# The last gate product of a two-block layer: steps between weight splits, partial sums kept in PSUM banks, the last block product by token block

## The chip, the cores and the metric

One core of a Trainium2 chip. The metric is device time in microseconds, the median of several runs. All times below are microseconds unless marked ns. The engines are named as in the profile: PE (TensorE, matmul), PEld (its weight loads), DVE (VectorE), ACT (ScalarE), POOL (GpSimd), SP (SyncE, which only issues transfers here).

## What is computed

Two layers on 512 tokens of width 2048, in float32. The first is a recurrence beside latent attention, the second sparse attention beside spatial gating. Only the end of the second layer changes:

```python
def second_block(x, p, ..., w_ple, w_ple_gate, final_g):
    ...
    x = x + merged @ w_out[l]
    x = x + jax.nn.sigmoid(x @ w_ple_gate[l]) * (p[l] @ w_ple[l])
    return rms_norm_2(x, final_g)

def rms_norm_2(x, g):
    xf = x.astype(jnp.float32)
    y = xf * lax.rsqrt(jnp.mean(xf * xf, axis=-1, keepdims=True) + EPS)
    return (y * g.astype(jnp.float32)).astype(x.dtype)
```

`x @ w_ple_gate` is 512x2048 by 2048x2048. `p @ w_ple` was computed earlier and lies in DRAM (`ple_d`).

## The kernel before

**Splitting.** A float32 weight block comes by DMA as `wraw`, ACT copies it into `whi` (a rounded format), DVE subtracts to get `wlo`. The same is done with the left operands. `mm3` then makes three matmuls, hi*hi, lo*hi and hi*lo, into one bank. A weight block of 128x2x512 is a *unit*; the list of all units is the `spine`. At each unit the program issues up to `LD = 4` fetches and `LS = 3` splits ahead.

**Seven block products.** The last product is done by a scheme of Strassen's kind, for two *pairs* p of column blocks, c = 2p and 2p + 1, 512 columns each. The left operand is cut in four quarters: two halves of the tokens (rows) by two halves of the inner dimension. Per pair there are seven block products, in the order `PROD = ("1","7","6","2","5","3","4")`. The left operands are the *forms* `F[q, k]`: sums of quarters (through `fs`), split. The weights' sums were made earlier by accumulating DMAs of POOL (`ws0x...`). Each product has four units, each unit 12 matmuls of 128x512: two token blocks j, two k, three of `mm3`. A product of token blocks j = 0, 1 has one bank per j (`pg1`, `pg7`, ...).

**Putting together.** `after_prod(p, q, j)` runs when the bank of (q, j) is done: `q1` is a copy of product 1 by ACT; `w = P6 - q1`; `q1 + P2` is a result; then `e = P5 + w`, `c22 = e - P7` is a result, `w = P7 - w`; `e + P3` and `w + P4` are results. A result is one 128x512 block (token block b of 4, column block c of 4) of the gate's argument. `gated` takes it on: tanh on ACT (`tgate`), two `stt` on DVE (with `plel`, which is p @ w_ple, and with `x3`, the residual x), a square with a sum into `ssq` on ACT. `scaled` multiplies `x3` by the final gain `fg` on DVE. In the code all of that is one piece: the whole of it stands in the queues of ACT and DVE where `after_prod` is called, with no split of weights between its steps.

**Order.** Work beside the spine is written as generators (`sides`); each `yield` names tiles, and `pump` goes on with a generator when a clock of estimates says that those are ready by then and that DVE and ACT are not too far behind PE. The list of instructions so found is then fixed by hand-made dependencies for every engine, so each engine's queue holds exactly that order.

**The end.** `finish(b, sums)` sums the squares of a token block, takes the reciprocal root by integer and Newton steps of 128x1 on DVE (tile `part`), scales the four column blocks of `x3` (ACT and DVE) and issues four output DMAs, from the queues of SP, ACT, SP and POOL. For token blocks 2 and 3, `part_gen` sums three of the four squares ahead. Product 4 of pair 1 is last (`last_product`). Its units are kept until all four are there; then j = 0 is computed 512 wide, j = 1 as two halves of 256, each half into a bank of its own:

```python
            for s in (slice(0, 512),) if j == 0 else (slice(0, 256), slice(256, 512)):
                ps = bank("pg4")[:, s]
```

In the rows, L285 is `tt` (DVE, two tensors), L304 `stt` (DVE, tensor, scalar and tensor), L294 and L296 `ts`, L316 `act`, L322 `mm`, L330 `dma`. After the change these are L283, L302, L292 and L294, L314, L321 and L329. The banks are named `pg` in the rows, with all buffers under one name; `q` is `q1`, `c` is `c22`, `x` is `x3`.

Of the kernel before, what the change touches and what calls it, by code (L numbers as in the profile page):

```python
# [12 lines left out]
OP = mybir.AluOpType  # L13
# [68 lines left out]
THIN = False  # L82
# [154 lines left out]
class Unit:  # L237
    def __init__(self, src, shape, mm, pre=None, hold=1, half=False, thin=False):


        self.src, self.shape, self.mm, self.pre, self.hold, self.half = src, shape, mm, pre, hold, half
        self.thin = thin
        self.raw = self.hi = self.lo = None


def emit(ctx, tc, I, out):
# [74 lines left out]
    def mm(o, l, r, start, stop_):  # L321
        T.matmul(o, l, r, start=start, stop=stop_)  # L322
# [18 lines left out]
    def mm3(o, lh, ll, rh, rl, start=False, stop_=False):  # L341
        mm(o, lh, rh, start, False)
        mm(o, lh, rl, False, False)
        mm(o, ll, rh, False, stop_)
# [1073 lines left out]
    done = {"oa": [], "ob": [], "sg": [], "x2": 0}  # L1418
# [622 lines left out]
    def form(q, k, x):  # L2041
        t = slot([128, 2, 256], "F" + q, F32R)
        act(t[:, 0], x, AF.Copy)
        yield [t]
        tt(t[:, 1], x, f(t[:, 0]), OP.subtract)
        F[q, k] = t

    def early_forms(k):
        x11, _, x21, x22 = quarters(k)
        yield [x22]  # L2050
        yield from form("1", k, x11)
# [5 lines left out]
        yield from form("6", k, s[:, 1])  # L2057

    def late_forms():
        for k in range(8):  # L2060
# [62 lines left out]
    def gated(b, c, src, s=slice(0, 512), end=False):  # L2123

        x = x3[b, c][:, s]
        t = slot([128, 512], "tgate")[:, s]
        act(t, src, AF.Tanh, scale=0.5)
        stt(t, t, 1.0, pl_[b, c][:, s], OP.add, OP.mult)
        stt(x, t, 0.5, x, OP.mult, OP.add)
        o = ssq[:, b, c:c + 1]  # L2130
        if end:
            o = small("sqe")[:, 0:1]
            stt(t, x, 1.0, x, OP.mult, OP.mult, accum_out=o)
        else:
            act(t, x, AF.Square, accum_out=o)
        return o

    def scaled(b, c):
        x = x3[b, c]
        tt(x, x, pl_["fg", c], OP.mult)  # L2140

    def after_prod(p, q, j):

        c = 2 * p
        ps = acc[q, j] if q == "7" else acc.pop((q, j))
        if q == "1":
            t = tmp["1", j] = slot([128, 512], "q1")
            act(t, ps, AF.Copy)
        elif q == "6":
            w = tmp["w", j] = slot([128, 512], "wq")  # L2150
            tt(w, ps, tmp["1", j], OP.subtract)
        elif q == "2":
            t = tmp.pop(("1", j))
            tt(t, ps, t, OP.add)
            gated(j, c, t)
        elif q == "5":
            e, t, w, p7 = slot([128, 512], "eq"), slot([128, 512], "c22"), tmp["w", j], acc.pop(("7", j))
            tmp["e", j] = e
# [249 lines left out]
```

## Time and profile before

| what | value |
|---|---|
| median of 3 runs | 2417.43 (2416.79 to 2417.78) |
| the profiled execution | 2413.85 |
| its span | 2412.0 |
| mean granted clock of PE | 0.992 |
| PE busy in the span | 2349.8 (97%) |
| DVE, ACT, POOL busy | 1543.5 (64%), 971.2 (40%), 290.5 (12%) |
| the stage that changes: first matmul to the end of the span | 2200.29 to 2412.0 |

The page's rows give, for an engine, its busy time and share; a mean over the whole span says little of the last stage, so the rows further down are read from that stretch alone. In a timeline row, the first number is the start from the span's start, the second the time taken, and the bracket behind it the idle time of that engine just before and what ended it.

### The profile page before, as it was taken

The numbers are of one execution on the slowest core, as the hardware profiler recorded it, in microseconds if no ns is written. First come the engines' busy times: TensorE is split into PE (matmuls) and PEld (weight loads), VectorE is DVE, ScalarE is ACT, GpSimd is POOL, SyncE is SP. The second block draws the span as 40 slices with busy tenths as digits, with TensorE's granted clock in tenths as the row PEclk, the third lists the DMA queues.
The fourth block names the chain that finished last, engine by engine and source line by source line (L and its number), as shares of the span: only waits on it lengthen the run. The fifth ranks groups of instructions, "written<-read, shape, count | busy, mean of one in ns | idle before, by whom it ended". The sixth has DMA issues, their size and how long they took to land.

```text
span 2412.0 us, 30852 instructions
## 1 busy us (share of the span) xinstructions
PE 2349.8 (97%) x11323; PEld 1965.0 (81%) x11323; DVE 1543.5 (64%) x2928; ACT 971.2 (40%) x1785; POOL 290.5 (12%) x432
## 2 busy tenths in 40 slices
PE   8999999999999999999999999999999999999895
PEld 6778889888888987888888888888888888888674
DVE  6777988788855377468887347776243444335766
ACT  6333366555543343344444235444232222224443
POOL 0000031432312002000000100001012000111110
PEclk9999999999999999999999999999999999999897
DMA  9976732432355346434444634435456433445563
GB/s 347 362 258 241 248 124 71 131 125 94 123 183 165 104 151 173 146 114 123 126 114 136 170 109 123 119 114 143 130 195 220 128 114 113 132 141 194 186 233 131
DMA packets 124167, 383.10 MB, mean 159 GB/s; under 512 B 16542, under 2 KB 16836, under 8 KB 123504
## 3 DMA queue, kind: packets, MB, share of 16 engines
q1 hardware_dynamic: 94896, 273.41, 34.7%
q0 software_dynamic: 28256, 106.58, 15.0%
q8 instruction: 89, 1.46, 0.2%
q10 hardware_dynamic: 864, 1.14, 0.1%
q14 instruction: 62, 0.51, 0.1%
HBM read 343.32 MB, written 71.30 MB: 172 GB/s over the span
## 4 chain that ended last, share of the span: by engine, by line
PE 53%; issue 6%; DVE 3%; ACT 1%; POOL 1%; DMA 0%; POOLq 0%; DVEq 0%; ACTq 0%
PE pch L322 45%; PE pO L322 2%; PE psc L322 2%; PE pPT L326 1%; PE pg L322 1%; DVE wlo L285 1%; ACT whi L316 0%; DVE cA L285 0%; PE pcs L322 0%; PE px L326 0%; DMA w1r<-in_cmp_w_v_dram 0%; DVE vx L304 0%; POOL x L330 0%; POOL plel L330 0%; PE psv L322 0%
## 5 line engine op out<-in xcount | busy, mean ns | idle before, releaser
L285 DVE TENSOR_TENSOR wlo<-wraw,whi 128x1024 fp32r<-128x1024 f32 (+5 forms) x421 | 498.0, 1184 | 190.6 <-ACT whi L316 188.1
L316 ACT ACTIVATE whi<-wraw 128x1024 fp32r<-128x1024 f32 (+5 forms) x423 | 424.2, 1013 | 321.8 <-PE pch L322 120.4
L322 PE MATMUL pch<-h2h,whi 128*128 128x512 f32 x1216 | 483.2, 397 | 0.0
L322 PE MATMUL pch<-h2h,wlo 128*128 128x512 f32 x1216 | 474.9, 391 | 0.0
L322 PE MATMUL pch<-h2l,whi 128*128 128x512 f32 x1216 | 474.5, 390 | 0.0
L322 PEld LDWEIGHTS pch<-h2h,wlo 128*128 128x128 f32 x1216 | 228.2, 188 | 48.4
L322 PEld LDWEIGHTS pch<-h2l,whi 128*128 128x128 f32 x1216 | 228.9, 188 | 41.0
L322 PEld LDWEIGHTS pch<-h2h,whi 128*128 128x128 f32 x1216 | 228.6, 188 | 41.0
L322 PE MATMUL pg<-whi,F 128*128 128x512 f32 (+1 forms) x464 | 149.4, 403 | 21.3 <-ACT whi L316 14.6
L316 ACT ACTIVATE P<-psc,sm 128x512 f32<-128x512 f32 (+3 forms) x160 | 83.7, 527 | 134.1 <-DVE sm L308 103.8
L322 PEld LDWEIGHTS pg<-whi,F 128*128 128x128 f32 x464 | 91.4, 200 | 43.4 <-ACT whi L316 17.2
L322 PE MATMUL pp<-hh,whi 128*128 128x512 f32 x320 | 126.0, 394 | 0.2 <-DVE acc L285 0.2
L322 PE MATMUL pp<-hh,wlo 128*128 128x512 f32 x320 | 124.7, 390 | 0.0
L322 PE MATMUL pp<-hl,whi 128*128 128x512 f32 x320 | 124.6, 389 | 0.0
L322 PE MATMUL pch<-mgh,whi 128*128 128x512 f32 x256 | 101.1, 395 | 0.0
L322 PE MATMUL pch<-mgh,wlo 128*128 128x512 f32 x256 | 99.9, 390 | 0.0
L322 PE MATMUL pch<-mgl,whi 128*128 128x512 f32 x256 | 99.6, 389 | 0.0
L322 PE MATMUL pch<-oh,whi 128*128 128x512 f32 x256 | 99.6, 389 | 0.0
L322 PE MATMUL pch<-ol,whi 128*128 128x512 f32 x256 | 99.6, 389 | 0.0
L322 PE MATMUL pch<-oh,wlo 128*128 128x512 f32 x256 | 99.6, 389 | 0.0
L322 PE MATMUL pg<-wlo,F 128*128 128x512 f32 (+1 forms) x232 | 93.8, 404 | 4.2 <-DVE wlo L285 4.2
L316 ACT ACTIVATE PTh<-pPT 128x512 fp32r<-128x512 f32 (+1 forms) x120 | 59.6, 529 | 90.9 <-PE pPT L326 88.5
(526 smaller groups left out, 4602.0 us busy)
## 6 DMA issues: line engine op xcount, KB each, us to landing
wraw<-in_w_in_dram SPq DMA_DIRECT2D x199, 512.0 KB, 3.6
wada<-in_w_mod_dram SPq DMA_DIRECT2D x128, 256.0 KB, 5.4
wraw<-in_w_out_dram SPq DMA_DIRECT2D x64, 512.0 KB, 3.6
wgate<-in_w_gate_dram SPq DMA_DIRECT2D x64, 256.0 KB, 4.6
wraw<-in_w_ple_gate_dram SPq DMA_DIRECT2D x24, 512.0 KB, 3.6
ws0x<-in_w_ple_gate_dram POOLq DMA_DIRECT2D x16, 512.0 KB, 7.6
ws1x<-in_w_ple_gate_dram POOLq DMA_DIRECT2D x16, 512.0 KB, 6.4
sg<-mg POOLq DMA_DIRECT2D x32, 256.0 KB, 2.6
```

The costliest lines, as they stand in the source:

```text
L285: V.tensor_tensor(o, a, b, op=op)
L316: A.activation(o, a, fn, **k)
L322: T.matmul(o, l, r, start=start, stop=stop_)
L326: T.transpose(o, a, i)
```

## The change

The last stage is written anew in four respects.

- *Generators.* `after_prod` now only copies (`q1`, `wq`) or spawns a generator (`from_2`, `from_5`, `from_3`, `from_4`); `gated` yields between tanh, `stt` and square. The gains `fg` on the columns of pair 0 are a generator too (`first_gains`), and `finish` of any block waits for its end. `finish` of blocks 0 and 1 is spawned when their four squares are noted (`nsum`).
- *Sums in the banks.* Form 1 is made with the scale -1, and products add up in a bank: 1, 6, 5 in bank `b`, 7 and 4 in `e`, 2 in `a`, 3 in `c`, with a start only for 1, 7, 2, 3. ACT copies what is needed on the way (`q1`, `wq`, `eq`), and DVE makes one addition or subtraction per result. Per pair and j, ACT has two copies more, DVE three operations fewer.
- *Form 2* of the first `EARLY2 = 4` k is made with the early forms, while `merged @ w_out` still runs.
- *The last product* is computed as its units come, token block 0 first; then token block 1 in two halves of 256, which are now two halves of one bank.

The part that goes with `thin` (never switched on) is dropped as well and left out here.

```diff
@@ -79,7 +79,7 @@
 SEGS = ((0, 0), (8, 1024), (16, 3136))
 EARLY = (0, 1, 8, 9)
 VGL = (((4656, 5016),), ((5016, 5376),), ((5376, 5680), (2560, 2608)))
-THIN = False
+EARLY2 = 4
 SUMS = 150
@@ -318,8 +316,9 @@
-    def mm(o, l, r, start, stop_):
-        T.matmul(o, l, r, start=start, stop=stop_)
+    def mm(o, l, r, start, stop_, on=False):
+        T.matmul(o, l, r, start=start, stop=stop_, skip_group_check=on)
@@ -2038,26 +2037,31 @@
         a, c = x2r[k], x2r[k + 8]
         return a[:, 0:256], c[:, 0:256], a[:, 256:512], c[:, 256:512]
-    def form(q, k, x):
+    def form(q, k, x, scale=1.0):
         t = slot([128, 2, 256], "F" + q, F32R)
-        act(t[:, 0], x, AF.Copy)
+        act(t[:, 0], x, AF.Copy, scale=scale)
         yield [t]
-        tt(t[:, 1], x, f(t[:, 0]), OP.subtract)
+        if scale == 1.0:
+            tt(t[:, 1], x, f(t[:, 0]), OP.subtract)
+        else:
+            stt(t[:, 1], x, scale, f(t[:, 0]), OP.mult, OP.subtract)
         F[q, k] = t
     def early_forms(k):
-        x11, _, x21, x22 = quarters(k)
+        x11, x12, x21, x22 = quarters(k)
         yield [x22]
-        yield from form("1", k, x11)
+        yield from form("1", k, x11, -1.0)
         s = slot([128, 2, 256], "fs")
         tt(s[:, 0], x11, x21, OP.subtract)
         tt(s[:, 1], s[:, 0], x22, OP.add)
         yield [s]
         yield from form("7", k, s[:, 0])
         yield from form("6", k, s[:, 1])
+        if k < EARLY2:
+            yield from form("2", k, x12)
     def late_forms():
-        for k in range(8):
+        for k in range(EARLY2, 8):
             yield
             yield from form("2", k, quarters(k)[1])
         for k in range(8):
@@ -2120,63 +2124,84 @@
         dma("G", pl_[b, c], ple_d[b][c])
         dma("G", x3[b, c], x2_d[:, b, c * 512:(c + 1) * 512])
-    def gated(b, c, src, s=slice(0, 512), end=False):
+    def gated(b, c, src, s=slice(0, 512), end=None):
+        yield [src, x3[b, c], pl_[b, c]]
         x = x3[b, c][:, s]
         t = slot([128, 512], "tgate")[:, s]
         act(t, src, AF.Tanh, scale=0.5)
+        yield [t]
         stt(t, t, 1.0, pl_[b, c][:, s], OP.add, OP.mult)
         stt(x, t, 0.5, x, OP.mult, OP.add)
-        o = ssq[:, b, c:c + 1]
-        if end:
-            o = small("sqe")[:, 0:1]
-            stt(t, x, 1.0, x, OP.mult, OP.mult, accum_out=o)
-        else:
-            act(t, x, AF.Square, accum_out=o)
-        return o
-    def scaled(b, c):
-        x = x3[b, c]
-        tt(x, x, pl_["fg", c], OP.mult)
+        if end is not None:
+            stt(t, x, 1.0, x, OP.mult, OP.mult, accum_out=end)
+            return
+        yield [x]
+        act(t, x, AF.Square, accum_out=ssq[:, b, c:c + 1])
+        if c > 1 and (b < 2 or c == 3):
+            tt(x, x, pl_["fg", c], OP.mult)
+        pl_.pop((b, c))
+        nsum[b] += 1
+        if b < 2 and nsum[b] == 4:
+            yield [ssq]
+            sides.spawn(finish(b, ()))
+        if b > 1 and nsum[b] == 3:
+            sides.spawn(part_gen(b))
+    nsum = [0] * TB
+    def first_gains():
+        for c in range(2):
+            for b in range(TB):
+                yield [x3[b, c]]
+                tt(x3[b, c], x3[b, c], pl_["fg", c], OP.mult)
+        done["gains"] = True
     def after_prod(p, q, j):
         c = 2 * p
-        ps = acc[q, j] if q == "7" else acc.pop((q, j))
         if q == "1":
             t = tmp["1", j] = slot([128, 512], "q1")
-            act(t, ps, AF.Copy)
+            act(t, acc["b", j], AF.Copy)
         elif q == "6":
-            w = tmp["w", j] = slot([128, 512], "wq")
-            tt(w, ps, tmp["1", j], OP.subtract)
-        elif q == "2":
-            t = tmp.pop(("1", j))
-            tt(t, ps, t, OP.add)
-            gated(j, c, t)
-        elif q == "5":
-            e, t, w, p7 = slot([128, 512], "eq"), slot([128, 512], "c22"), tmp["w", j], acc.pop(("7", j))
-            tmp["e", j] = e
-            tt(e, ps, w, OP.add)
-            tt(t, e, p7, OP.subtract)
-            tt(w, p7, w, OP.subtract)
-            gated(2 + j, c + 1, t)
+            t = tmp["w", j] = slot([128, 512], "wq")
+            act(t, acc["b", j], AF.Copy)
+        elif q in "25":
+            sides.spawn({"2": from_2, "5": from_5}[q](j, c))
         elif q == "3":
-            t = tmp.pop(("e", j))
-            tt(t, ps, t, OP.add)
-            gated(j, c + 1, t)
+            sides.spawn(from_3(j, c))
         elif q == "4":
-            t = tmp.pop(("w", j))
-            tt(t, ps, t, OP.add)
-            gated(2 + j, c, t)
-        if p == 1:
-            if q in "253":
-                b, cc_ = {"2": (j, c), "5": (2 + j, c + 1), "3": (j, c + 1)}[q]
-                scaled(b, cc_)
-            if q == "3":
-                sides.spawn(finish(j, ()))
-            if q == "5":
-                sides.spawn(part_gen(2 + j))
+            sides.spawn(from_4(j, c))
+    def from_2(j, c):
+        t, ps = tmp.pop(("1", j)), acc.pop(("a", j))
+        yield [t, ps]
+        tt(t, ps, t, OP.subtract)
+        yield from gated(j, c, t)
+    def from_5(j, c):
+        e, t, ps, p7 = slot([128, 512], "eq"), slot([128, 512], "c22"), acc.pop(("b", j)), acc["e", j]
+        tmp["e", j] = e
+        yield [ps]
+        act(e, ps, AF.Copy)
+        yield [e, p7]
+        tt(t, e, p7, OP.subtract)
+        done["c22"] += 1
+        yield from gated(2 + j, c + 1, t)
+    def from_3(j, c):
+        t, ps = tmp.pop(("e", j)), acc.pop(("c", j))
+        yield [t, ps]
+        tt(t, ps, t, OP.add)
+        yield from gated(j, c + 1, t)
+    def from_4(j, c):
+        t, ps = tmp.pop(("w", j)), acc.pop(("e", j))
+        yield [t, ps]
+        tt(t, ps, t, OP.subtract)
+        yield from gated(2 + j, c, t)
+    CH = {"1": "b", "6": "b", "5": "b", "7": "e", "4": "e", "2": "a", "3": "c"}
     OUT = {"2": (0, 0), "5": (2, 1), "3": (0, 1), "4": (2, 0)}
     def prod_pre(p, q, u):
@@ -2193,9 +2218,10 @@
                 for c in range(4):
                     t = pl_["fg", c] = slot([128, 512], "fg")
                     dma("G", t, bcast(I["final_g_2"], 512, c * 512))
-            if p == 1 and q in "762":
-                for b, c in {"7": ((0, 0), (1, 0)), "6": ((2, 1), (3, 1), (0, 1)), "2": ((1, 1), (2, 0), (3, 0))}[q]:
-                    scaled(b, c)
+            if p == 1 and q == "7":
+                sides.spawn(first_gains())
+            if q == "4":
+                sides.until(lambda: done["c22"] == 2 * p + 2)
             if q in OUT:
                 sides.until(lambda: done["x2"] == KT)
                 b, c = OUT[q]
@@ -2211,18 +2237,17 @@
             def mmf(hi, lo):
                 if last_:
                     held[u] = (hi, lo)
-                    if u == 3:
-                        yield from last_product(held)
+                    yield from last_product(u, held)
                     return
                 for j in range(2):
-                    if u == 0:
-                        acc[q, j] = bank("pg" + q)
-                    ps = acc[q, j]
+                    if u == 0 and q in "1723":
+                        acc[CH[q], j] = bank("pg" + CH[q])
+                    ps = acc[CH[q], j]
                     t = slice(j * 128, (j + 1) * 128)
                     for kk in range(2):
                         w = F[q, 2 * u + kk]
-                        mm3(ps, w[:, 0, t], w[:, 1, t], hi[:, kk, :], lo[:, kk, :], u == 0 and kk == 0,
-                            u == 3 and kk == 1)
+                        mm3(ps, w[:, 0, t], w[:, 1, t], hi[:, kk, :], lo[:, kk, :], q in "1723" and u == 0 and kk == 0,
+                            u == 3 and kk == 1, q in "654")
                         yield
                     if u == 3:
                         after_prod(p, q, j)
@@ -2232,26 +2257,32 @@
                         F.pop((q, 2 * u + kk))
             return Unit(wsrc(p, q, u), (2, 512), mmf, pre=prod_pre(p, q, u),
         return [mk(u) for u in range(4)]
-    def last_product(ws):
-        for j in range(2):
-            t = slice(j * 128, (j + 1) * 128)
-            sums = []
-            for s in (slice(0, 512),) if j == 0 else (slice(0, 256), slice(256, 512)):
-                ps = bank("pg4")[:, s]
-                for k in range(8):
-                    hi, lo = ws[k // 2]
-                    w = F["4", k]
-                    mm3(ps, w[:, 0, t], w[:, 1, t], hi[:, k % 2, s], lo[:, k % 2, s], k == 0, k == 7)
-                    yield
+    def last_product(u, ws):
+        def part_(j, ks, s, end):
+            ps = acc["e", j][:, s]
+            for k in ks:
+                hi, lo = ws[k // 2]
+                w, t = F["4", k], slice(j * 128, (j + 1) * 128)
+                mm3(ps, w[:, 0, t], w[:, 1, t], hi[:, k % 2, s], lo[:, k % 2, s], False, k == 7, True)
+                yield
+            if end is not None:
                 x = tmp["w", j][:, s]
-                tt(x, ps, x, OP.add)
-                sums.append(gated(2 + j, 2, x, s, s.stop == 512))
-            sides.spawn(finish(2 + j, sums))
-            yield
+                tt(x, ps, x, OP.subtract)
+                for _ in gated(2 + j, 2, x, s, end):
+                    pass
+        e0 = small("sqe")
+        yield from part_(0, (2 * u, 2 * u + 1), slice(0, 512), e0[:, 0:1] if u == 3 else None)
+        if u == 3:
+            sides.spawn(finish(2, (e0[:, 0:1],)))
+            e1, e2 = small("sqe"), small("sqe")
+            yield from part_(1, range(8), slice(0, 256), e1[:, 0:1])
+            yield from part_(1, range(8), slice(256, 512), e2[:, 0:1])
+            sides.spawn(finish(3, (e1[:, 0:1], e2[:, 0:1])))
     def part_gen(b):
         yield [ssq]
@@ -2262,6 +2293,8 @@
     def finish(b, sums):
+        while "gains" not in done:
+            yield
         yield
         if sums:
             ms = part[b]
```

On ACT, pair 1, from the results of product 2 on (`whi<-wraw` is a weight's copy; `tgate<-q` the tanh, `tgate,ssq<-x` the square). Before:

```order
L316 ACTIVATE whi<-wraw 128x1024 x12
L316 ACTIVATE tgate<-q_20105 128x512
L316 ACTIVATE tgate,ssq<-x_20275 128x512
L316 ACTIVATE tgate<-q_20113 128x512
L316 ACTIVATE tgate,ssq<-x_20279 128x512
L316 ACTIVATE whi<-wraw 128x1024 x4
```

and after:

```order
L314 ACTIVATE whi<-wraw 128x1024 x4
L314 ACTIVATE tgate<-q_20097 128x512
L314 ACTIVATE whi<-wraw 128x1024 x2
L314 ACTIVATE tgate,ssq<-x_20265 128x512
L314 ACTIVATE tgate<-q_20105 128x512
L314 ACTIVATE whi<-wraw 128x1024 x2
L314 ACTIVATE tgate,ssq<-x_20269 128x512
L314 ACTIVATE eq<-pgb 128x512
L314 ACTIVATE whi<-wraw 128x1024
L314 ACTIVATE eq<-pgb 128x512
```

The four activations of the two results now have copies of weights between them.

On PE, where the second half of token block 3 begins in the last product (`[waits DVE_49]` is a wait on a semaphore of DVE that PE has not seen reached yet). Before:

```order
L322 MATMUL pg4_20669<-whi_20593,F4_19993 128x256
L322 MATMUL pg4_20669<-wlo_20594,F4_19993 128x256
L322 MATMUL pg4_20669<-whi_20593,F4_19993 128x256
L322 MATMUL pg4_20700<-whi_20526,F4_19872 128x256
L322 MATMUL pg4_20700<-wlo_20527,F4_19872 128x256
```

and after:

```order
L321 MATMUL pge_20121<-whi_20574,F4_19907 128x256
L321 MATMUL pge_20121<-wlo_20575,F4_19907 128x256
L321 MATMUL pge_20121<-whi_20574,F4_19907 128x256
L321 MATMUL pge_20121<-whi_20507,F4_19796 128x256 [waits DVE_49]
L321 MATMUL pge_20121<-wlo_20508,F4_19796 128x256
```

The order on PE is the same; the second half goes to the same bank, and its first matmul has a wait for the instruction `wq<-pge,wq 128x256` of the first half.

On DVE at the end of the program (`part` is the reciprocal root of one token block, `x_19580` and `x_19584` are column blocks of token blocks 0 and 1, `wlo<-wraw,whi` a split). Before:

```order
L285 TENSOR_TENSOR wlo<-wraw,whi 128x1024 x2
L308 TENSOR_REDUCE part<-ssq 128x1
...
L304 SCALAR_TENSOR_TENSOR part<-part 128x1 x6
L294 TENSOR_SCALAR x_19584<-x_19584,part 128x512
L285 TENSOR_TENSOR wq<-pg_20597,wq 128x512
```

and after (`x_20447` and `x_20451` are results of product 3; the rows left out behind these are the gates of the two halves):

```order
L283 TENSOR_TENSOR wlo<-wraw,whi 128x1024
L302 SCALAR_TENSOR_TENSOR tgate<-tgate,plel 128x512
L302 SCALAR_TENSOR_TENSOR x_20447<-tgate,x_20447 128x512
L302 SCALAR_TENSOR_TENSOR tgate<-tgate,plel 128x512
L302 SCALAR_TENSOR_TENSOR x_20451<-tgate,x_20451 128x512
L283 TENSOR_TENSOR wq<-pge,wq 128x512
L302 SCALAR_TENSOR_TENSOR tgate<-tgate,plel 128x512
L302 SCALAR_TENSOR_TENSOR x_20552<-tgate,x_20552 128x512
L302 SCALAR_TENSOR_TENSOR tgate,sqe<-x_20552 128x512
L283 TENSOR_TENSOR x_20447<-x_20447,fg 128x512
L283 TENSOR_TENSOR wq<-pge,wq 128x256
...
L292 TENSOR_SCALAR x_19918<-x_19918,part 128x512
...
L292 TENSOR_SCALAR x_19583<-x_19583,part 128x512
...
L292 TENSOR_SCALAR x_19922<-x_19922,part 128x512
...
L292 TENSOR_SCALAR x_19587<-x_19587,part 128x512
```

The `finish` of blocks 0 and 1, ahead of the last product's sums before, now stands behind them, in the order 2, 0, 3, 1 of the four last rows; two gates of product 3 and one gain stand ahead of the read of the first half.

## Rows read from the trace of the kernel before

**Rows 1.** Waits of PE, 2200 to 2412: total us, times, longest.

```profile
PE pg L322 <- ACT whi L316: 14.6, 6, 4.7
PE pg L322 <- DVE wlo L285: 4.2, 6, 0.8
PE pg L322 <- DVE F L285: 4.0, 1, 4.0
PE pg L322 <- ACT F L316: 2.7, 2, 2.0
```

**Rows 2.** Busy time by window: us, PE, PEld, DVE, ACT, POOL, clock, DMA, GB/s.

```profile
2040.00:2200.00 160.00, 160.00 (x734) 132.42 (x733) 56.32 (x77) 44.83 (x64) 16.52 (x26) 1.00 0.45 135
2200.00:2250.00 50.00, 49.90 (x222) 40.96 (x221) 39.47 (x67) 25.98 (x43) 6.08 (x11) 1.00 0.69 236
2250.00:2300.00 50.00, 38.25 (x135) 29.34 (x136) 34.64 (x52) 23.74 (x43) 7.10 (x14) 0.86 0.57 185
2300.00:2350.00 50.00, 46.66 (x203) 37.66 (x201) 32.55 (x37) 22.42 (x28) 6.84 (x13) 1.00 0.73 248
2350.00:2395.00 45.00, 34.06 (x144) 27.23 (x143) 32.99 (x66) 18.51 (x28) 1.09 (x2) 0.85 0.37 128
```

**Rows 3.** Timeline around the end of product 2 of pair 1.

```profile
2346.46 0.69 DVE L304 SCALAR_TENSOR_TENSOR tgate<-tgate,plel 128x512 f32<-128x512 f32 x1 [0.70 <-ACT tgate L316]
...
2347.91 0.63 ACT L316 ACTIVATE tgate<-x 128x512 f32<-128x512 f32 x1 [1.49 <-DVE x L304]
...
2348.54 2.94 ACT L316 ACTIVATE whi<-wraw 128x1024 fp32r<-128x1024 f32 x3
...
2349.64 0.50 PE L322 MATMUL pg<-whi,F 128*128 128x512 f32 x1 [2.00 <-ACT whi L316]
```

**Rows 4.** Timeline of PE: the stage's first matmul, steady stretches, its end.

```profile
2200.29 0.39 PE L322 MATMUL pg<-whi,F 128*128 128x512 f32 x1
...
2310.30 0.39 PE L322 MATMUL pg<-wlo,F 128*128 128x512 f32 x1
...
2317.10 0.39 PE L322 MATMUL pg<-wlo,F 128*128 128x512 f32 x1
...
2385.32 0.63 PE L322 MATMUL pg<-wlo,F 128*128 128x512 f32 x1
...
2386.60 0.63 PE L322 MATMUL pg<-wlo,F 128*128 128x512 f32 x1
...
2388.77 0.40 PE L322 MATMUL pg<-whi,F 128*128 128x256 f32 x2
...
2394.16 0.28 PE L322 MATMUL pg<-whi,F 128*128 128x256 f32 x1
```

**Rows 5.** Timeline of DVE and ACT at the end of the program.

```profile
2384.87 0.15 DVE L308 TENSOR_REDUCE part<-ssq 128x1 f32<-128x4 f32 x1
...
2389.98 0.69 DVE L285 TENSOR_TENSOR wq<-pg,wq 128x512 f32<-128x512 f32 x1
...
2396.40 0.42 DVE L285 TENSOR_TENSOR wq<-pg,wq 128x256 f32<-128x256 f32 x1
...
2398.63 0.08 DVE L304 DVE_READ_ACCUMULATOR tgate<-x 128x1 f32 x1
...
2404.49 0.48 DVE L294 TENSOR_SCALAR x<-x,part 128x512 f32<-128x512 f32 x1
...
2404.99 0.72 ACT L316 ACTIVATE x<-x,part 128x512 f32<-128x512 f32 x1 [0.45 <-ACT x L316]
```

**Rows 6.** Transfers from 2380 to 2412, GB/s in 40 slices.

```profile
GB/s 0 0 0 0 0 0 0 0 0 0 87 369 371 358 241 374 346 371 113 13 0 0 0 0 0 0 0 87 379 310 369 233 394 323 366 161 0 0 0 0
```

**Rows 7.** Groups of instructions, 2200 to 2412: count, busy us, mean ns, idle before.

```profile
L316 ACT ACTIVATE whi<-wraw 128x1024 fp32r<-128x1024 f32 x53 | 54.5, 1051 | 25.3 <-DMA wraw<-ws1x 8.0 <-DMA wraw<-in_w_ple_gate_dram 7.7 <-DVE wlo L285 4.1
L285 DVE TENSOR_TENSOR wlo<-wraw,whi 128x1024 fp32r<-128x1024 f32 x54 | 65.6, 1223 | 29.1 <-ACT whi L316 28.2 <-DVE wlo L285 0.2
L285 DVE TENSOR_TENSOR F<-x1l,F 128x256 fp32r<-128x256 f32 x17 | 6.7, 418 | 0.0
```

More of the change, by code (lines that the diff above doesn't have):

```diff
@@ L237, with __init__ @@
 class Unit:
-    def __init__(self, src, shape, mm, pre=None, hold=1, half=False, thin=False):
+    def __init__(self, src, shape, mm, pre=None, hold=1, half=False):
         self.src, self.shape, self.mm, self.pre, self.hold, self.half = src, shape, mm, pre, hold, half
-        self.thin = thin
         self.raw = self.hi = self.lo = None
@@ L339, in split, with mm3 @@
             stt(lo, src, scale, f(hi), OP.mult, OP.subtract)
[L341 to L344, printed above, removed]
+    def mm3(o, lh, ll, rh, rl, start=False, stop_=False, on=False):
+        mm(o, lh, rh, start, False, on)
+        mm(o, lh, rl, False, False, on)
+        mm(o, ll, rh, False, stop_, on)
     def rsqrt(x, n, name="rs"):
@@ L1417, in emit @@
     c1 = 0.7978845608028654
-    done = {"oa": [], "ob": [], "sg": [], "x2": 0}
+    done = {"oa": [], "ob": [], "sg": [], "x2": 0, "c22": 0}
     def gelu2_gen(x, **k):
@@ L2234, in mk @@
             return Unit(wsrc(p, q, u), (2, 512), mmf, pre=prod_pre(p, q, u),
-                        hold=(4 if u == 3 else 0) if last_ else 1, thin=THIN and p == 0 and u % 2 == 1)
+                        hold=(4 if u == 3 else 0) if last_ else 1)
         return [mk(u) for u in range(4)]
-    def last_product(ws):
-        for j in range(2):
-            t = slice(j * 128, (j + 1) * 128)
-            sums = []
-            for s in (slice(0, 512),) if j == 0 else (slice(0, 256), slice(256, 512)):
-                ps = bank("pg4")[:, s]
-                for k in range(8):
-                    hi, lo = ws[k // 2]
-                    w = F["4", k]
-                    mm3(ps, w[:, 0, t], w[:, 1, t], hi[:, k % 2, s], lo[:, k % 2, s], k == 0, k == 7)
-                    yield
-                x = tmp["w", j][:, s]
-                tt(x, ps, x, OP.add)
-                sums.append(gated(2 + j, 2, x, s, s.stop == 512))
-            sides.spawn(finish(2 + j, sums))
-            yield
+    def last_product(u, ws):
[7 more added lines that the diff above has]
+            if end is not None:
+                x = tmp["w", j][:, s]
+                tt(x, ps, x, OP.subtract)
[9 more added lines that the diff above has]
+            sides.spawn(finish(3, (e1[:, 0:1], e2[:, 0:1])))
     def part_gen(b):
@@ L2322, in split_next @@
             gtt(u.lo, u.raw, f(u.hi), OP.subtract)
-        elif u.thin:
-            act(u.hi, u.raw, AF.Copy)
-            act(u.lo, f(u.hi), AF.Copy, scale=-1.0)
-            G.dma_start(u.lo, u.raw, accum_op=OP.add, max_dma_last_dim=4096)
-            clock.dma("G", u.lo, u.raw)
         else:
```

## The prediction

> **What bounds the kernel now.** The change touches the last stage alone, so I looked for the stretch in which it runs. On PE's timeline its first matmul, `pg<-whi,F`, starts at 2200.29 and its last ends at 2394.44; the span ends at 2412.0 [rows 4]. The windows come next: up to 2250 PE is busy nearly all the time, in the three after that it has 38.25 of 50, 46.66 of 50 and 34.06 of 45 us, and in the first and third of these the granted clock is 0.86 and 0.85 [rows 2]. So PE sets the pace in this stage, with holes in it, and the reader should see that holes and low clock come together. The waits say who makes the holes: 25.5 us in all, 14.6 of them behind ACT's copy `whi<-wraw`, 4.2 behind DVE's `wlo` and 6.7 behind the forms `F` [rows 1].
>
> One hole read closely gives the cause. The step that follows a block product is one piece in the queues: DVE waits 0.70 for the tanh, ACT waits 1.49 for DVE's two products before it squares, and only behind the square does ACT start three copies of weights in a row; PE has waited 2.00 us when the first is done, at 2349.64 [rows 3]. The splits are not too slow: one costs 1.05 us of ACT and 1.22 us of DVE [rows 7], against 2.7 us that PE needs for its 12 matmuls. They are only late.
>
> The stage's time, taken apart: from 2310.30 to 2317.10 lie 30 matmuls of 128x512, 0.227 each, and from 2388.77 to 2394.16 lie 45 of 128x256, 0.12 each [rows 4]. The stage has 648 and 48 of them: 146.9 + 5.8 = 152.7 us. PE's stretch is 2394.44 - 2200.29 = 194.15. What is left, 41.5, is 25.5 of waits and 16.0 of other loss; the clock columns account for 0.14 x 50 + 0.15 x 45 = 13.8 of that [rows 2]. At the lower level (1.2 of 2.4 GHz) three matmuls take 1.28 us, 0.427 each [rows 4]. Behind PE's end 17.6 us follow: the last half's gate, two `finish`, and outputs. The profiled execution took 2413.85 us with a span of 2412.0; the median is 2417.43, so I carry the difference of spans over to the median.
>
> **The change, part by part.** *Steps between splits.* After product 2 of pair 1 ACT now has two copies of weights between each tanh and its square, and single ones around the copies `eq`, where before one atomic row of four activations stood. A hop of DVE or ACT then holds up one split, not all of them. Three units of lead are 3 x 2.7 = 8.2 us, and a block's chain (0.69 + 0.63 + 0.70 + 1.49 and what is between, [rows 3]) is about half of that. The waits for forms (6.7) are of the same kind: the forms 2 and 5 of pair 0 queue behind the pieces of product 6 and 2. So of the 25.5 us I keep 0.6: for the form 5 of the last k in pair 0 and the last unit's `wlo`. With the holes the low clock goes, 13.8. Of the 2.2 left over I keep 0.5 (hand-overs and the last transposes). What is late next is DVE: in a product of pair 1 it carries four splits (4.9) and two blocks of four steps at 0.69 (5.5), 10.4 of PE's 10.9 us. That cover is thin, and it is my first rival.
>
> *Sums in the banks.* Twelve DVE additions of 0.69 us [rows 5] go, 8.3 us, and eight ACT copies of some 0.63 come, 5.0 us. ACT is busy 90.65 of 195 us in the four windows of the stage [rows 2]; each copy is read two products, or one, before its bank is written again, 10.9 us at least. I cost it at nothing. Should DVE stay the tight engine, those 8.3 us are what it gains, which is why I don't count them again.
>
> *Form 2 of four k moved forward*: four copies and four subtractions of 0.42 us [rows 7] land in the stage before, where DVE is busy 56.32 of 160 us and PE all of it [rows 2]. That idle time hides them: nothing; with DVE full there it would be 4 x 0.42 = 1.7 us. POOL's and SP's queues keep their order, so no load and no sum of weights moves in its queue; loads issue when a buffer is free, and these come free with the splits.
>
> *The last product.* The order on PE is unchanged, but the second half of block 3 now writes into the same bank as the first and its first matmul waits for DVE's `wq<-pge` of the first half. Before it had its own bank and started at once: the 256-wide matmuls run at 0.12 through both halves [rows 4]. DVE reaches that read late. With no other loss the 512-wide part ends at 2200.29 + 146.9 + 1.1 = 2348.2. DVE then still has the two gates of product 3, about 1.4 us of them; then `wq` (0.69), tanh (0.63 with ACT free), two products and a squared sum (3 x 0.69) and 0.2 between, 3.6; one gain, 0.69; the read itself, 0.42: 2354.4. PE's first half takes 24 x 0.12 = 2.9 and ends at 2351.1. So it waits 3.3 to 3.4 us. After holes of 2.00 and 4.7 us PE ran at the lower level [rows 3, 4], so I run the second half at 0.24 a matmul: 5.8 instead of 2.9. Bounds: with no backlog and no gain on DVE the read would still come 3.6 + 0.4 after the 512-wide part and leave 1.1; with twice the backlog 4.8; to each 0 or 2.9 of clock is added. I take 3.4 + 2.9 = 6.3, since the orders show both the gates and the gain ahead of the read.
>
> The Trainium skill says, in "Perfetto Trace Analysis", section "Matmuls" under "Optimizing Tensor Performance", that independent matmul groups should rotate through different banks, so that one is read out while the next is computed. It speaks against this part of the change: by it the time is the one above, and if two halves of one bank did not get in each other's way it would be 6.3 us less. The trace before shows the rotation at work, not what its absence costs.
>
> *The tail.* Before, `finish` of blocks 0 and 1 stood on DVE ahead of the last product's sums and were done during it (2384.87 to 2389.98, 5.1 us); only blocks 2 and 3 came behind (2398.71 to 2404.97, 6.3 us) [rows 5]. Now all four stand behind the last half's gate, in the order 2, 0, 3, 1: 11.4 us of DVE. Ahead of them, from PE's end, the gate of a half: 0.1 + 2.3 (2396.40 to 2398.71). Behind them, 7.0 as before (2404.97 to 2412.0), and 1.3 more because block 1 ends on three ACT scalings of 0.72 with a 0.45 gap, where block 3 had two. That is 22.1 against 17.6: 4.5 lost. All 4.2 MB of outputs now leave there; at about 360 GB/s [rows 6] that is 11.7 us, inside the 11.4 + 7.0, so it costs 0 to 3 and I take 0.
>
> **Sum.** PE's end: 2200.29 + 152.7 + 0.5 + 0.6 + 6.3 = 2360.4. Span: 2360.4 + 22.1 = 2382.5, which is 29.5 less than 2412.0. Predicted median: 2417.43 - 29.5 = 2388.
>
> **Rivals.** *Holes remain, because DVE is nearly full.* 10.4 of 10.9 us leave little for hops of 0.70 that still fall on its queue, and the lead of 8.2 us is eaten in the four products 2, 5, 3, 4 of each pair. For it: DVE's load; against it: twelve additions are gone. If 5 to 10 of the 25.5 us stay, each brings its share of low clock (13.8 / 25.5 = 0.54): 7.7 to 15.4 more, 2396 to 2404. The sign stays.
>
> *Slower: the chain of each block reaches PE.* The generators cut the chain, but on in-order queues each cut is a place where ACT and DVE can wait on each other behind a split. If the two hops (0.70 + 1.49 = 2.19 us, [rows 3]) of 14 blocks fall on PE in full, that is 30.7 us, with the clock 47: 2435. It eats the gain from 1.37 us a block on, and is over 0.2% slower (some 5 us, about what a measurement of this kernel can tell) from 1.6. Against it: before, with no split between a block's steps at all, six waits for `whi` and six for `wlo` were what reached PE [rows 1].
>
> *Better: the second half does not wait.* If DVE is ahead by then, or the clock stays up, the last product costs up to 6.3 less: 2382.
>
> *The change does not do what it says*: the order on ACT and DVE does show the steps between the splits, so I give that nothing of its own.
>
> **How the numbers follow.** Forecast 0.64 (2383 to 2394); holes remain 0.20; better 0.08; slower 0.05; between these, no difference that can be told, 0.03. The range 2380 to 2405 holds the forecast, the better case and nearly all of the first rival, and leaves out some 0.15. Faster 0.92, same 0.03, slower 0.05.
>
> **What would show it.** Right: between 2200 and some 2350 PE waits under 2 us in all and the granted clock stays at 1.00; one wait of about 3.4 us behind DVE's `wq` 24 matmuls before the end, 0.24 a matmul after it; PE's end near 2360; then four runs of Newton steps on DVE and 22 us to the end of the span. Wrong: waits for `whi` or `wlo` of over 1 us at several places (first rival, and by their number and size the second), no wait at the second half (third), a tail above 25 us (outputs bound by the queues), or a clock of 0.85 in a window without holes.

## The result and the profile after

The changed kernel takes 2384.31 us, the median of four runs (2383.53 to 2385.32), against 2417.11 of before: ratio 0.9865, with an interval of 0.9848 to 0.9882. The profiled execution has a span of 2382.8; the prediction had 2382.5.

Waits of PE in the last stage, after (total us, times, longest); they answer to [rows 1]:

```profile
PE pgb L321 <- ACT F L314: 2.4, 1, 2.4
PE pge L321 <- DVE wq L283: 1.7, 1, 1.7
```

No wait for `whi` or `wlo` is left: 25.5 us have become 4.1. The windows of [rows 2] in the stage, the last one shorter (us, PE, PEld, DVE, ACT, POOL, granted clock, DMA share, GB/s):

```profile
2200.00:2250.00 50.00, 50.00 (x225) 41.36 (x224) 36.36 (x61) 27.27 (x42) 5.55 (x10) 1.00 0.67 228
2250.00:2300.00 50.00, 47.57 (x204) 38.96 (x203) 41.60 (x60) 30.85 (x54) 12.30 (x23) 0.97 0.80 286
2300.00:2350.00 50.00, 50.00 (x222) 41.41 (x221) 37.97 (x49) 28.26 (x38) 2.15 (x4) 1.00 0.68 228
2350.00:2365.00 15.00, 10.54 (x62) 9.51 (x60) 10.80 (x26) 3.11 (x8) 0.00 (x0) 0.89 0.01 1
```

The clock stays at 1.00 where PE has no hole. The window with the form's wait has 0.97, the one with the last product 0.89 (it reaches 2.7 us past PE's end). The place of [rows 3], the results of product 2 in pair 1, now reads so on ACT and DVE:

```profile
2324.60 0.69 DVE L283 TENSOR_TENSOR q<-pga,q 128x512 f32<-128x512 f32 x1 [1.10 <-PE pga L321]
...
2325.33 0.63 ACT L314 ACTIVATE tgate<-q 128x512 f32<-128x512 f32 x1 [3.08 <-DVE q L283]
...
2325.87 1.99 ACT L314 ACTIVATE whi<-wraw 128x1024 fp32r<-128x1024 f32 x2
...
2329.53 0.63 ACT L314 ACTIVATE tgate<-x 128x512 f32<-128x512 f32 x1 [1.67 <-DVE x L302]
```

ACT still idles before the square (1.67 here, 1.49 before), but two copies of weights have gone ahead of it, so PE no longer waits for that. The hops are where they were; what stands between them has changed.

PE's first matmul of the stage, its two waits, and its last matmul:

```profile
2201.44 0.39 PE L321 MATMUL pgb<-whi,F 128*128 128x512 f32 x1
...
2256.89 0.80 PE L321 MATMUL pgb<-whi,F 128*128 128x512 f32 x1 [2.43 <-ACT F L314]
...
2357.74 0.39 PE L321 MATMUL pge<-whi,F 128*128 128x256 f32 x1 [1.75 <-DVE wq L283]
...
2361.87 0.41 PE L321 MATMUL pge<-whi,F 128*128 128x256 f32 x1
```

The end on DVE, as in [rows 5], and the transfers from 2350 to the end in 40 slices, as in [rows 6]:

```profile
2353.21 0.68 DVE L283 TENSOR_TENSOR wq<-pge,wq 128x512 f32<-128x512 f32 x1
...
2357.27 0.42 DVE L283 TENSOR_TENSOR wq<-pge,wq 128x256 f32<-128x256 f32 x1
...
2362.32 0.42 DVE L283 TENSOR_TENSOR wq<-pge,wq 128x256 f32<-128x256 f32 x1 [2.19 <-PE pge L321]
...
2364.50 0.08 DVE L302 DVE_READ_ACCUMULATOR tgate<-x 128x1 f32 x1
...
2375.47 0.48 DVE L292 TENSOR_SCALAR x<-x,part 128x512 f32<-128x512 f32 x1
```

```profile
GB/s 0 0 0 0 20 0 0 0 0 0 0 0 0 0 0 0 0 0 0 0 0 0 362 317 392 225 385 317 362 382 382 322 365 372 387 360 185 0 0 0
```

Ahead of its last read DVE waits 2.19 us for PE. The four finishes run one behind the other from 2364.58 to 2375.95, 11.4 us, and all outputs leave in one stretch.

### The profile page after: what moved, and what is told of

It reads as the page before. It is cut to its first block, busy times and chain, and to the rows that moved or that the text cites. A ratio compares the mean times of both kernels' runs of the same rounds, so it can differ in the third digit from the quotient of the medians.

```text
span 2382.8 us, 30848 instructions
## 1 busy us (share of the span) xinstructions
PE 2339.3 (98%) x11323; PEld 1960.3 (82%) x11323; DVE 1534.0 (64%) x2918; ACT 974.7 (41%) x1791; POOL 291.9 (12%) x432
## 4 chain that ended last, share of the span: by engine, by line
PE 58%; DVE 3%; issue 1%; ACT 1%; DMA 1%; POOL 0%; ACTq 0%; DVEq 0%; POOLq 0%
PE pch L321 46%; PE pgb L321 2%; PE pO L321 2%; PE psc L321 2%; PE pge L321 2%; PE pPT L325 1%; DVE wlo L283 1%; PE pgc L321 1%; PE pga L321 0%; ACT whi L314 0%; DVE cA L283 0%; PE pcs L321 0%; PE px L325 0%; DMA w1r<-in_cmp_w_v_dram 0%; DVE vx L302 0%
## 5 line engine op out<-in xcount | busy, mean ns | idle before, releaser
L283 DVE TENSOR_TENSOR mg<-pch,R 128x512 f32<-128x512 f32 x32 | 22.1, 690 | 116.4 <-PE pch L321 116.4
L306 DVE TENSOR_REDUCE sm<-psc 128x1 f32<-128x512 f32 (+3 forms) x160 | 78.6, 491 | 5.5
L283 DVE TENSOR_TENSOR PTl<-pPT,PTh 128x512 fp32r<-128x512 f32 (+1 forms) x120 | 68.1, 594 | 9.8 <-ACT PTh L314 9.6
```

The lines of the kernel that those rows point to most:

```text
L283: V.tensor_tensor(o, a, b, op=op)
L306: V.tensor_reduce(o, a, AX.X, op, **k)
```

## The experiments

The first matmul of the stage comes between 2200.05 and 2204.43 in the profiled executions, though its work ahead hardly differs: the first `pp` matmul, some 50 us after the start, is already 47.7 in one and 51.0 in another. So beside the medians (the executions of one kernel lie 0.5 to 6.4 us apart) I compare the *stage*: from its first matmul to the end of the span, in one profiled execution of each kernel. The changed kernel's two traces differ by 1.5 us in it, so less than that it does not tell. Each kernel is the changed one with the edit that is named, and each ratio is to before as measured beside it (medians of 2416.01 to 2417.42). "PE waits" is the sum in the stage.

| kernel | median | ratio to before (interval) | stage | PE waits |
|---|---|---|---|---|
| before | 2417.11 | | 211.7 | 25.5 |
| the changed kernel | 2384.31 | 0.9865 (0.9848 to 0.9882) | 181.4 | 4.1 |
| the same again | 2386.10 | 0.9870 (0.9856 to 0.9885) | 179.9 | 4.0 |
| steps in one piece | 2419.82 | 1.0012 (1.0003 to 1.0021) | 215.2 | 26.5 |
| the square alone apart | 2396.11 | 0.9913 (0.9898 to 0.9928) | 192.0 | 14.1 |
| sums on DVE | 2384.34 | 0.9864 (0.9849 to 0.9878) | 179.6 | 1.0 |
| form 2 late | 2385.79 | 0.9866 (0.9850 to 0.9883) | 180.7 | 4.6 |
| own bank for the last half | 2384.36 | 0.9863 (0.9848 to 0.9878) | 178.9 | 1.9 |
| steps alone | 2385.72 | 0.9875 (0.9858 to 0.9891) | 181.6 | 1.2 |
| two more DVE additions | 2405.89 | 0.9954 (0.9938 to 0.9971) | 201.0 | 12.5 |
| another end | 2380.14 | 0.9849 (0.9834 to 0.9863) | 175.6 | 2.0 |
| another end, again | 2381.10 | 0.9850 (0.9836 to 0.9865) | 175.7 | 2.0 |
| another end, gains on DVE | 2381.85 | 0.9855 (0.9841 to 0.9870) | 175.8 | 2.0 |
| another end, forms 5 first | 2381.37 | 0.9855 (0.9840 to 0.9869) | 176.2 | 2.5 |

### Steps in one piece

```diff
-            sides.spawn({"2": from_2, "5": from_5}[q](j, c))
+            at_once({"2": from_2, "5": from_5}[q](j, c))
         elif q == "3":
-            sides.spawn(from_3(j, c))
+            at_once(from_3(j, c))
         elif q == "4":
-            sides.spawn(from_4(j, c))
+            at_once(from_4(j, c))
+    def at_once(g):
+        for _ in g:
+            pass
```

> The changed kernel, but the generators that follow products 2, 5, 3 and 4 are run through at once where they were spawned, so their steps stand in one piece again; sums in the banks, early form 2 and the last product stay. Theory (the gain is the steps between the splits): holes at the product ends come back, some 20 us of waits for whi and wlo and about 0.54 of that in low clock, less what the changed kernel has there: 2405 to 2414. Rival (the gain is the twelve DVE additions less): 2384 to 2392, no wait over 1 us for whi.

Measured: 2419.82. The whole gain is gone, and a little more. Its longest waits of PE:

```profile
PE pgc L321 <- ACT whi L314: 5.7, 2, 3.1
PE pgb L321 <- ACT whi L314: 4.8, 3, 2.2
PE pge L321 <- ACT whi L314: 4.7, 1, 4.7
PE pge L321 <- DVE F L283: 4.1, 1, 4.1
PE pge L321 <- DVE wq L283: 3.2, 1, 3.2
...
```

The granted clock falls with them again (0.80 here, 0.97 in the changed kernel):

```profile
2250.00:2300.00 50.00, 39.32 (x131) 29.62 (x130) 31.98 (x48) 23.98 (x43) 6.97 (x13) 0.80 0.58 180
```

15.2 us behind `whi`, in six waits, as before (14.6 in six, [rows 1]), with the lighter DVE, the sums in the banks and the early form 2 all in place. So without the steps between the splits the other parts bring nothing, and the rival (fewer additions) falls. The time is 6 us above what I expected at most: I had let the other parts keep something, and they keep nothing; the wait at the last half (3.2) comes on top.

### The square alone apart

```diff
+        yield "square"
         yield [x]
...
+    def to_square(g):
+        r = next(g)
+        while r != "square":
+            r = next(g)
+        sides.spawn(g)
```

Each spawn of `from_2`, `from_5`, `from_3` and `from_4` goes through `to_square`, so addition, tanh and products stand in one piece.

> The changed kernel, but of each result's chain the addition, the tanh and the two products are again in one piece where product ends; the square and what is behind it stay a step between the splits. Theory (the holes are made by the last hop, DVE's two products to ACT's square, behind which the copies of weights stand): copies start some 2.1 us earlier than with all in one piece, so holes of 2 us go and those of 3 to 4.7 shrink to 1 to 2.6; 5 to 8 us of waits in all, 2391 to 2400. Rival (each hop counts alike): 2405 to 2412. Rival (any single cut is enough): 2383 to 2387.

Measured: 2396.11 (executions from 2392.04 to 2398.44), in the theory's range; the waits are 14.1 us in all, where the theory had 5 to 8.

```profile
PE pge L321 <- DVE wq L283: 3.4, 1, 3.4
PE pge L321 <- ACT whi L314: 2.5, 1, 2.5
PE pgb L321 <- DVE wlo L283: 2.3, 2, 1.1
PE pgc L321 <- DVE wlo L283: 1.5, 2, 1.1
PE pgb L321 <- ACT F L314: 1.4, 1, 1.4
...
PE pge L321 <- DVE wlo L283: 1.1, 1, 1.1
```

Waits for `whi` fall from 15.2 to 3.0 (the 2.5 of this list and one of 0.5). One cut, at the hop that ACT waits longest for (1.49 in [rows 3]), brings 23.7 of the 35.5 us between the kernel in one piece and the changed one; a single cut at another hop was not tried. What stays for the splits is mostly `wlo`, 4.9 us in five waits, four of them of 1.1: DVE's own hop, 0.70 of waiting for the tanh and then the two products, which the theory had left out. The last half takes 3.4 and the forms 2.8.

### Sums on DVE, form 2 late, the steps alone

*Sums on DVE*: each product its own bank, form 1 with the scale 1, and

```diff
-            act(t, acc["b", j], AF.Copy)
+            tt(t, acc.pop(("6", j)), tmp["1", j], OP.subtract)
...
-        act(e, ps, AF.Copy)
+        tt(e, ps, w, OP.add)
         yield [e, p7]
         tt(t, e, p7, OP.subtract)
+        tt(w, p7, w, OP.subtract)
```

> The changed kernel, but each product has a bank of its own and the sums are made on DVE as before (twelve additions more, eight ACT copies less); the steps stay between the splits. The halves of the last product have banks of their own too. Theory (steps between the splits): holes of 3 us at most besides the form's, and no wait at the last half: 2381 to 2389. Rival (DVE was the tight engine and the additions less are the gain; 10.4 of 10.9 us becomes 11.8): waits for wlo in pair 1 of 8 us and more, 2394 to 2405.

*Form 2 late*: `EARLY2 = 0`.

> The changed kernel with form 2 of all k in the late forms (EARLY2 = 0). Theory: it only shortens the queue of late forms; without it PE waits for forms in pair 0 for some 2.4 + 4 x 0.8 us, with the low clock 3 to 6 more: 2387 to 2391. Rival (the forms had room): same as the changed kernel within 1 us.

*The steps alone* takes both together, and puts the finishes of blocks 0 and 1 back ahead of the last product's sums.

> The kernel before, as nearly as can be, with the steps between the splits alone: a bank and DVE sums for each product, form 2 all late, finishes of blocks 0 and 1 ahead of the last product's sums, halves in banks of their own. Theory (the steps are the whole gain, the other parts of the change give nothing or take a little): not slower than the changed kernel, 2380 to 2385. Rival (the steps need the lighter DVE or the early forms): 2390 and more.

Measured: 2384.34, 2385.79 and 2385.72; stages of 179.6, 180.7 and 181.6 against 181.4 and 179.9 of the changed kernel. Neither the sums in the banks nor the early form 2 can be told from nothing, and the steps without them bring it all. For form 2 late the theory (2387 to 2391) missed and the rival fits, as near as two medians of the changed kernel (2384.31 and 2386.10) can say; the steps alone lie 0.7 above their theory's range and far below the rival's. One part of the change is in all of these kernels, the last product computed as its units come: without the steps it brings nothing (steps in one piece), and whether the steps need it was not tried. The kernel with sums on DVE, whose last halves have banks of their own, has a single wait left, and the kernel with form 2 late waits for a form about as long as the changed one:

```profile
PE pg L321 <- ACT F L314: 1.0, 1, 1.0
```

```profile
PE pgb L321 <- ACT F L314: 2.7, 1, 2.7
PE pge L321 <- DVE wq L283: 1.9, 1, 1.9
```

In the steps alone PE ends at 2357.1, some 5 us earlier than in the changed kernel, and the span does not: DVE carries its work to the end, and with the finishes' scalings ahead of it on ACT it waits for the tanh:

```profile
2363.75 0.69 DVE L302 SCALAR_TENSOR_TENSOR tgate<-tgate,plel 128x512 f32<-128x512 f32 x1 [1.95 <-ACT tgate L314]
```

### An own bank for the last half

```diff
+        if c == 2 and j == 1:
+            w = tmp["w", j][:, 256:512]
+            tt(w, p7[:, 256:512], w, OP.subtract)
...
-            ps = acc["e", j][:, s]
+            own = s.start == 256
+            ps = bank("pg4")[:, s] if own else acc["e", j][:, s]
```

> The changed kernel, but the second half of token block 3 of the last product goes to a bank of its own; a 128x256 subtraction on DVE after product 5 prepares for it. Theory: PE does not wait there (1.7 us) and the clock stays up (1.6 us); PE ends 3.3 earlier, but DVE comes to the last read only at about 2360.1 instead of 2362.3, so 2.2 are gained: 2382. Rival (PE's end sets the end): 3.3 gained, 2381. Rival (DVE sets the end there in either case): 0 gained, 2384.3.

Measured: 2384.36, no change in the median, as the second rival had it; the wait for `wq` is gone, and the stage is 178.9, which is 2.4 less than the first trace of the changed kernel and 1.0 less than the second. The two traces differ at just this place. After its wait of 1.7 the first ran at 0.89 in that window; the second waited 1.8 and did not slow down:

```profile
2350.00:2365.00 15.00, 11.12 (x71) 9.85 (x69) 12.20 (x23) 4.79 (x10) 0.00 (x0) 1.00 0.00 1
```

DVE's rows say what can be won here: at its last read it waits for PE, 2.19 us in the first trace of the changed kernel and 0.78 in the second, and in this kernel not at all. From there on its own chain sets the end, however early PE is done. So PE's share is worth some 1 to 2.4 us in the traces, the theory's 2.2 among them, and the medians do not show it.

### Two more DVE additions in each result

```diff
         stt(x, t, 0.5, x, OP.mult, OP.add)
+        for _ in range(2 if end is None else 0):
+            tt(t, t, x, OP.add)
```

> The changed kernel with two more DVE additions of 128x512 (of no use) in each of the 14 results that are squared on ACT: 28 x 0.69 = 19.3 us more of DVE, 2.8 us more in a product. Theory (the steps fit because three units of lead, 8.2 us, carry a product in which DVE has more to do than PE): waits of PE of 3 to 10 us, 2388 to 2400. Rival (10.4 of 10.9 us is the limit and every us more falls on PE): 15 us of waits and more, with the clock 2407 to 2415. Rival (DVE has room): 2383 to 2387.

Measured: 2405.89, between the theory and the first rival; the stage is 19.7 longer than the changed kernel's first, about what was added (19.3). Of it 11.1 come ahead of PE's end and 8.6 behind.

```profile
PE pge L321 <- DVE wq L283: 5.4, 1, 5.4
PE pgb L321 <- ACT F L314: 4.2, 1, 4.2
PE pge L321 <- DVE wlo L283: 2.3, 2, 1.3
PE pgb L321 <- DVE F L283: 0.6, 1, 0.6
```

The lead does what the theory said for the splits: 2.3 us of waits. Forms take 4.8, the last half 5.4, and the granted clock from 2250 to 2300 is 0.93. Behind PE's end there are 29.1 us of tail instead of 20.5: the order found for this kernel puts the second gate of product 3 behind two finishes, and DVE also waits for ACT around it (1.91 and 2.63 us):

```profile
2386.21 0.68 DVE L302 SCALAR_TENSOR_TENSOR tgate<-tgate,plel 128x512 f32<-128x512 f32 x1
```

So this run does not price the cover of the splits cleanly. It shows that the splits take little of what is added to DVE; the rest is paid at the forms, at the last half and behind PE's end.

### Another end

Both blocks of the last product are 512 wide in their bank `e`. The end is one hand-written order: Newton steps and scalings of block 0, sum and tanh of block 2, Newton steps of block 1, sum and tanh of block 3, scalings of block 1, then the gates and the finishes of 2 and 3. The square of block 2 goes to ACT, two gains to POOL.

```diff
-            tt(x, x, pl_["fg", c], OP.mult)
+            (gtt if b < 2 and c == 3 else tt)(x, x, pl_["fg", c], OP.mult)
...
+        step(fin[0])
+        summed(0)
+        step(fin[1])
+        step(fin[1])
+        summed(1)
+        step(fin[1])
+        mixed(0)
+        e0, e1 = small("sqe"), small("sqe")
+        act(tg[0], x3[2, 2], AF.Square, accum_out=e0[:, 0:1])
+        mixed(1)
```

> The changed kernel with another end: both token blocks of the last product 512 wide in one bank each, the finishes of blocks 0 and 1 on DVE between the sums of the last product, two gains on POOL, one square on ACT. Theory (from the last splits on DVE sets the end, with 11.4 us of finishes behind the last gate): 5 to 6 us less from the stage's start to the end, 2378 to 2380. Rival (PE's end and the outputs' transfers set it): within 2 us of the changed kernel.

> The run with another end once more: 4 to 6 us less than the changed kernel of the same call (theory: DVE's order at the end), or within 2 (rival).

> The changed kernel once more beside the others: 2384.3, all theories; the PE wait at the last half and the wait for a form as in the first trace.

Measured: 2380.14 and 2381.10 against 2384.31 and 2386.10: 4 to 5 us in the medians, 4.2 to 5.8 in the stages. This is the fastest version here. PE ends at 2359.1 in the first of the two traces. From its first read of the last product to its last instruction DVE idles 3.9 us in the changed kernel's first trace (1.7 for the tanh, 2.19 for PE) and 2.4 in the second, and in this order not at all: more than half of the gain, as the theory had it. The rest goes with less work on DVE (one square is ACT's, nothing is cut in halves); of the parts of this end only the gains were tried by themselves.

*The gains back on DVE*: `gtt` becomes `tt` again.

> As the run with another end, but the two gains back from POOL to DVE (1.4 us of DVE). Theory (while POOL worked on them, DVE's six steps of 128x1 took 2.58 instead of 1.31 us, so nothing was won by it): the six steps take 1.31 again, time within 0.5 us of that run, 2380. Rival (DVE's slow stretch has another cause): the steps still take 2.6, 1.4 us more, 2381.5.

*Forms 5 ahead of forms 3* in the late forms, on top of the other end:

> As the run before, and in the late forms all eight forms 5 are made ahead of the forms 3. Theory (PE's wait of 2.4 us in product 5 of pair 0 is for forms 5 that stand behind forms 3, and costs some 1.5 us of low clock): 3.9 us less than the run before, 2374 to 2376, no wait of PE for a form. Rival (the wait moves to the forms 3 or 4): same as the run before.

Measured: 2381.85 and 2381.37. In the first the six steps take 1.31 again, as the theory had it (more in the last section). Its time does not decide: it is 1.7 and 0.8 us above the two runs of the other end, nearer to the rival's 2381.5, and the stages (175.8 against 175.6 and 175.7) are the same. In the second the rival was right: the wait for form 5 is gone, and waits for the forms 3 and 4 come in its place, of the same sum within half a us:

```profile
PE pge L321 <- DVE F L283: 0.9, 1, 0.9
PE pgc L321 <- ACT F L314: 0.8, 1, 0.8
PE pgc L321 <- DVE F L283: 0.8, 2, 0.4
```

The granted clock stays at 1.00 through these short waits, and still the stage is not shorter (176.2 and 175.6).

## Why the prediction was right, and where its terms were off

**The cause was right, and shown.** Holes at the product ends come from a result's chain standing in one piece in the queues of ACT and DVE. Put back into one piece, they return with their clock, and the time with them. The reason that they go fits the rows too: the splits' lead covers a hop once copies may pass it (two copies ahead of the square, and no wait of PE); the lead itself was not varied.

**The sum came out right by terms that miss in both directions.** Forecast stage 182.2, measured 181.4, in part by luck:

| term | forecast | first trace |
|---|---|---|
| PE's matmuls | 152.7 | 152.7 (taken as forecast) |
| waits for forms and splits | 0.6 | 2.4 |
| wait at the last half | 3.4 | 1.7 |
| low clock | 2.9 | 2.9 (1.5 at the form, 1.4 at the last half) |
| left over on PE | 0.5 | 1.1 |
| from PE's end to the end | 22.1 | 20.5 |

- *The form.* The place was named (form 5, pair 0, product 5), the size was four times too small, and its low clock (0.03 x 50 = 1.5) was missed. So the sign that I had set, under 2 us of waits and a clock of 1.00 up to 2350, was not met (2.4 and 0.97). I had taken the waits for forms to go with the pieces ahead of them; but the form has a chain of its own, in which ACT waits for DVE's sum `fs`, and with the forms 5 ahead of the forms 3 PE does not wait for it. Early form 2 shortens the wait little or not at all (2.7 without it, 2.4 and 2.2 with it).

```profile
2256.43 0.42 ACT L314 ACTIVATE F<-fs 128x256 fp32r<-128x256 f32 x1 [1.39 <-DVE fs L283]
```

- *The last half.* The backlog of DVE was the mis-sized term: 1.4 forecast; measured, `wq` starts at 2353.21, 0.1 behind the end of the last 512-wide matmul. Counted from the stage's start, PE came there 3.8 us later than forecast (the form's hole and its clock), DVE only 2.5. The chain behind it was right: 2353.21 to 2357.69 is 4.5, forecast 4.7. The low clock came only from 2358.8 on, so 1.4 of it (the 24 matmuls take 4.5 us here and 3.1 in the second trace), and none in the second trace; 2.9 was the upper end.
- *The rule on banks.* The Trainium skill's advice to rotate banks ("Perfetto Trace Analysis", section "Matmuls" under "Optimizing Tensor Performance") holds at this one place, where the next write comes straight behind: own banks take the wait away. Between products, where a bank is written again 10.9 us later or more, sharing cost nothing that can be seen: PE has no wait for a bank there, and the time is 2384.31 shared and 2384.34 with banks rotated (in a kernel that also has twelve more DVE additions).
- *The tail.* DVE's 11.4 was met to 0.1 us. Behind DVE's last instruction 6.9 us followed, not 8.3: I added 1.3 for the longer ACT chain, and the way from ACT's last scaling to the end became shorter instead (4.9 us, 6.3 before). DVE now spaces the outputs over one stretch where [rows 6] has two bursts; that this is the reason was not tried.
- *Finishes moved to the end.* The arithmetic was right, the price was not: with them ahead again (the steps alone) nothing is won. What sets the end is DVE's chain from the last product on, with what it waits for in it: the other end, which has no such wait and less work on DVE, takes 4 to 5 us less.

**The median.** The stage shrank by 30.4, forecast 29.5; the medians by 32.8. I carried the difference of spans over to the median, from an execution of before (2412.0) that was faster than 26 of the 27 measured beside the experiments (2411.7 to 2418.3). The spans differ by 29.2 us and the medians by 32.8, which is nearly the whole way from the forecast 2388 to 2384.31.

**The rivals.** Holes from a full DVE did not come: DVE was as full as reckoned (10.43 us busy in the 10.9 from 2335.2 to 2346.1, a product of pair 1), and PE had no wait for a split. The slower case's mechanism (both hops of every block reaching PE) did not occur; what a whole piece costs is the run in one piece. "The change does not do what it says" is out. The better case is real in part: the second trace ran at full clock there.

## What to carry to other kernels

When the busiest engine waits for a producer that is not busy, look at what stands ahead of the awaited instruction in that producer's queue, and at what that in turn waits for. Cutting such a chain at its longest hop alone brought two thirds of the gain (no other single cut was tried); making the chain lighter brought nothing. Once the holes are gone, ask which engine sets the last 20 us: here PE ended 5 us earlier in one version and the time did not move.

## What the runs showed of the hardware

POOL and DVE got in each other's way. In the other end POOL makes two gains while DVE does Newton steps; the six steps with two tensor inputs take 2.58 us, while those with one, ahead of them, take their usual 0.15:

```profile
2353.36 2.88 POOL L287 TENSOR_TENSOR x<-x,fg 128x512 f32<-128x512 f32 x2 [47.61 <-ACT tgate L314]
...
2354.39 0.14 DVE L292 TENSOR_SCALAR part<-part 128x1 f32<-128x1 f32 x1
2354.57 2.58 DVE L302 SCALAR_TENSOR_TENSOR part<-part 128x1 f32<-128x1 f32 x6
```

The next six in the same trace, with no work on POOL beside them, take half of that, and so do the first six with the gains on DVE:

```profile
2359.00 1.31 DVE L302 SCALAR_TENSOR_TENSOR part<-part 128x1 f32<-128x1 f32 x6
```

```profile
2358.32 1.31 DVE L302 SCALAR_TENSOR_TENSOR part<-part 128x1 f32<-128x1 f32 x6
```

The Trainium skill ("SBUF — State Buffer", section "SBUF: two separate sides") says that a DVE instruction with two SBUF inputs and a POOL instruction that reads SBUF exclude each other for a whole instruction. The rows agree in kind and size: 1.27 us lost against 1.44 for one POOL instruction. POOL's help was worth 0.1 us of DVE's time here, since of 1.38 us taken off DVE 1.27 came back as waiting.

The other point is the clock: two executions of one program waited 1.7 and 1.8 us at the same place, and one ran the rest of the product in part at the lower level (24 matmuls in 4.5 us, 0.89 in the window), the other at 1.00 (3.1 us).
